# Value rows of a product-key expert layer: scaled and added by VectorE instead of ScalarE and GpSimd

## The chip, the cores and the metric

The kernel runs on one core of a Trainium2 chip. The metric is the device time of one execution in microseconds; lower is better. A run is given as the median of several executions. The profile is one execution, recorded by the hardware profiler; its times are counted from the first instruction. TensorE is called PE in the views, VectorE DVE, ScalarE ACT, GpSimd POOL, and SyncE, which only issues DMAs here, SP.

## The reference, cut to what matters

The program is two transformer blocks on 512 tokens of 1024 features. The change lies in the last part of the second block, a product-key expert layer with 16384 experts: each token takes 8 heads times 16 experts, each with a row of `peer_u` and a row of `peer_v`.

```python
def peer_ffn(h, peer_w_q, peer_keys_1, peer_keys_2, peer_u, peer_v):
    ...
    experts = (e1 * PEER_N_KEYS + e2).reshape(T, PEER_HEADS * PEER_TOPK)
    gates = jax.nn.softmax(sc.astype(jnp.float32), axis=-1)...
    def chunk_fn(args):
        hc, ec, gc = args
        u = peer_u[ec]
        act = jax.nn.gelu(jnp.einsum('cd,ced->ce', hc, u))
        return jnp.einsum('ce,ced->cd', gc * act, peer_v[ec])
...
h = layer_norm(ALPHA * h + peer_ffn(h, ...), ln2_g, ln2_b)
```

## The kernel before

All of the change is in `peer()` and its inner functions. The first 128 tokens are computed as the reference says, from gathered rows: `gather()` fetches, by indirect DMAs issued by GpSimd (L1940), one row for each of the 128 tokens at a time, first 128 times a row of u, then 128 times a row of v. Three row buffers of 128x1024 rotate; row n + 2 is fetched when row n is about to be used. A row of u is multiplied with the tokens and summed by VectorE in one pass (L1953). A row of v is scaled by ScalarE, in place (L1955), and then added to the sum by GpSimd (L1956).

The other 384 tokens go densely through all experts, 128 experts at a time. `up(j)` is a product of 24 matmuls (eight tiles of features, three float32r products each in `mm3`, L281 to L283) that gives the experts' activations (gelu, L1798). `weigh(j)` multiplies them with the gates: the gates lie in DRAM (`gd`, written by the stage before) and are loaded by `gload(c)` for eight j at once, three tiles `page` of 128x1024 for the three tiles of tokens. The multiplication (L1993) is done on VectorE for one tile of tokens at a time, and `split` then makes the exact pair (hi, lo) by a ScalarE copy (L287) and a VectorE subtraction (L288). The products with v run for c = 0 to 15 and, within c, for d = 0 to 7; each is again 24 matmuls, and its sum is added to the residual by `settle` (L2020) on VectorE. 128 such settles count the stage's progress. From c = 1 on each v product is followed by a u product, until the 97 tiles of u that are left are used up: that is a pair, some 97 times, and then single v products to the end.

The weights of every product come as 128x1024 chunks through `Stream`: SP loads them, ScalarE copies the upper part (L155), and the engine in `ws.rest` subtracts it (L157, the lower part, which the third matmul of a triple needs as its weights). In c = 0 `ws.rest` alternates GpSimd and VectorE; from c = 1 it is VectorE. In each d, after `settle`, `next(gat)` advances the gathered rows: by one in c = 0, three in c = 8, else two.

The program is written in this order, but a scheduler orders the instructions of each engine when the kernel is built, by what it holds to be ready; on the chip each engine then runs its instructions in that fixed order. After the last product the last layer norm of the dense tokens ends the program (L1487 to L1509).

Of the kernel before, what the change touches and what calls it, by code (L numbers as in the profile page):

```python
# [14 lines left out]
S = 512  # L15
# [10 lines left out]
# tiles of experts whose act runs beside the queries, the last best keys, the gates, and after them  # L26
# [24 lines left out]
class Arena:  # L51
    """Columns of tiles, given out and taken back in the order of the program."""
# [16 lines left out]
    def alloc(self, n, top=False):  # L69
        """top: for longer than this part of the program."""  # L70
# [35 lines left out]
class Pair:  # L106
    """A float32 array as the exact sum of two float32r arrays."""
# [9 lines left out]
class Stream:  # L117
    """Weights from DRAM in the order of their use: loaded ahead, split ahead.

    The order is what the program asked for when it was traced before (order None: nothing is ahead)."""  # L120
# [20 lines left out]
    def load(self, i):  # L141
        """Chunk i of the order, if there is room."""
        key, n = self.order[i]
        c = self.chunks[key][n]
        if not self.free:
            return False
        c[1] = self.free.pop(0)
        self.k.nc.sync.dma_start(c[1].ap, c[0])
        return True
# [26 lines left out]
    def get(self, key):  # L176
        """The next chunk of that key: (hi, lo), each [128, 1024], or what was loaded. One chunk is used at a time."""
# [31 lines left out]
def drain(*gens):  # L209
    """Runs generators side by side; each yields the time its step takes on the tensor engine."""  # L210
# [11 lines left out]
class K:  # L222
# [6 lines left out]
    # ---- memory  # L229
# [6 lines left out]
    def phase(self, f=0, r=0, turns=True):  # L236
        """The memory that the next part has beside the two arenas: f and r KB. turns: PSUM's banks are used in turn."""
# [40 lines left out]
    # ---- arithmetic  # L278
# [6 lines left out]
    def split(self, hi, lo, x):  # L285
        """hi + lo = x, exactly."""
# [19 lines left out]
    # ---- the program  # L306
# [123 lines left out]
    # ---- modulation: mod[p, tile, kind] = silu(c) @ ada_w + ada_b  # L430
    def ada_prep(self):
# [8 lines left out]
        # the two kinds' silu(c) in the first of 32 columns  # L440
# [3 lines left out]
        # kinds[p, h, k]: whether row p of four products of 32 rows is of half h and of kind k  # L444
# [6 lines left out]
    def ada(self, l, blocks=range(12)):  # L451
# [28 lines left out]
        for nb in blocks:  # L480
            ps = self.bank()
            for ch in range(4):
                w = self.ws.get(f"ada{l}")
                # four products side by side, each on 32 columns of the array: two tiles of features by two halves
# [12 lines left out]
    # ---- norm over features, replicated on all partitions: 1/sqrt(mean(x^2) + eps)  # L497
    def rstd(self, ps, n, cols, eps):
        """ps: sums; gives [128, cols] of 1/sqrt(sum/n + eps)."""
# [6 lines left out]
    def xs(self, k, seg):  # L506
        """Tile k of the residual, some of the tokens: the latents', or the context's from S on."""
# [3 lines left out]
    def tiles(self, h, W):  # L511
        """Tiles of W columns of the two parts of h."""
        return [(h.hi.ap[:, i : i + W], h.lo.ap[:, i : i + W]) for i in range(0, h.hi.n, W)]

    def norm_mod(self, l, j, seg, h):
        """h (tiles): the modulated norm of x, of some of the tokens."""
# [17 lines left out]
    def square(self, x, n, acc):  # L534
        """acc += x^2; acc None: a new one."""
# [9 lines left out]
    def squares(self, x, nk, acc, room):  # L545
        """acc = the sum of x's squared tiles."""
# [6 lines left out]
    def stat(self, k, seg):  # L553
        """Tile k of x is done: its squares are added for the next norm."""
# [3 lines left out]
    def norm(self, x, nk, n, eps=0, acc=None):  # L558
        """1/sqrt(mean over features of x^2 + eps) on all partitions, and two [128, n] to work in."""
# [12 lines left out]
    # ---- the hyena filter's transform at odd frequencies  # L572
    def hy_filter(self):
# [42 lines left out]
        for kind, ts in (("l", range(0, 4)), ("c", range(4, 6))):  # L616
            # h = hid @ w3, decayed: sums and differences of the two sides
# [25 lines left out]
            # 1/(L |h|) by channel  # L643
# [23 lines left out]
    def dft(self, kind, pa, pb, put):  # L667
        """put(f, cos part of pa, sin part of pb), both in PSUM, for each tile of frequencies."""
# [23 lines left out]
    # ---- keys of two heads: tiles 4 and 5 hold one head's each, with zeros in place of the other's features  # L692
# [9 lines left out]
    # ---- layer 0: hyena and windowed attention  # L702
    def mixer0(self, filt):
# [127 lines left out]
        # the tokens of y whose product is done make room for the next norm  # L831
# [899 lines left out]
    def peer(self):  # L1731
# [195 lines left out]
        for x in [keys, iota, sel] + stages + pair:  # L1927
            x.free()
# [584 lines left out]
```

## Time and profile before

| | |
|---|---|
| median of three runs | 4011.34 us (4011.12 to 4017.75) |
| span of the profiled execution | 3998.4 us |
| mean granted TensorE clock | 0.960 of full speed |
| settles of the expert stage (L2020) | 128, from 2903.6 to 3974.0 us |
| rows of u used (L1953) | 128, the last in the window from 3297.7 us |
| adds of rows of v (L1956) | 128, from 3320.1 to 3899.6 us |

The profile lists the span alone for its execution; the median lies 12.9 us above it, which is taken as the start and end around the first and last instruction. The expert stage is thus the last 1100 us, and within it four stretches can be told apart by the count of settles: c = 0 (8 settles, to 2944.8 us), the pairs beside rows of u (40, to 3297.7), the pairs beside rows of v (56, to 3863.1), and the last 24 settles (to 3974.7). The last layer norm takes the rest, to 3998.4.

### The profile page before, as it was taken

How to read it: one execution, taken by the hardware profiler on the slowest of the kernel's cores; microseconds unless marked ns; L12 is line 12 of the kernel's file. 1: busy time of each engine (PE TensorE's matmuls, PEld its weight loads, DVE VectorE, ACT ScalarE, POOL GpSimd, SP SyncE). 2: the span in 40 equal slices, each digit the busy share in tenths (PEclk: the TensorE clock that was granted, in tenths of full speed). 3: DMA queues.
4: the chain of work that ended last, by engine and by line, in shares of the span. 5: the costliest groups of instructions: out<-in, count | busy, mean ns of one | idle time of the engine just before them, and what ended most of it. 6: DMA issues, size and time to landing. Idle time of an engine off the chain costs nothing. (4 is left out here: it accounts for less than half of the span.)

```text
span 3998.4 us, 51340 instructions
## 1 busy us (share of the span) xinstructions
PE 3658.0 (91%) x20063; PEld 3210.7 (80%) x20063; DVE 2703.9 (68%) x4011; ACT 1597.4 (40%) x2504; POOL 1627.3 (41%) x885
## 2 busy tenths in 40 slices
PE   7999999999999999988999888977789998988988
PEld 4766688888878888877888678876788998988987
DVE  6533774434466365557445667999888889899895
ACT  5333452222253333335223554336433334555552
POOL 2222451000042433323001515667754447888880
PEclk8999999999999999999999988989999999999999
DMA  5355432221231222213233313225678887767763
GB/s 196 131 189 195 142 116 77 63 63 63 68 105 56 82 66 79 72 48 106 95 100 101 105 47 126 84 86 162 212 271 295 314 304 240 254 228 239 235 219 99
DMA packets 199599, 573.39 MB, mean 143 GB/s; under 512 B 17051, under 2 KB 67227, under 8 KB 199356
## 3 DMA queue, kind: packets, MB, share of 16 engines
q1 hardware_dynamic: 100224, 362.33, 27.9%
q0 software_dynamic: 49328, 181.73, 12.9%
q10 hardware_dynamic: 49804, 26.06, 2.3%
q8 instruction: 157, 2.57, 0.3%
q14 instruction: 86, 0.70, 0.1%
HBM read 539.64 MB, written 30.41 MB: 143 GB/s over the span
## 5 line engine op out<-in xcount | busy, mean ns | idle before, releaser
L157 POOL TENSOR_TENSOR ra<-fa,ra 128x1024 fp32r<-128x1024 f32 x234 | 591.3, 2533 | 1616.7 <-ACT ra L155 1502.0
L155 ACT CAST ra<-fa 128x1024 fp32r<-128x1024 f32 x591 | 618.0, 1047 | 1293.8 <-PE P L282 499.2
L157 DVE TENSOR_TENSOR ra<-fa,ra 128x1024 fp32r<-128x1024 f32 x357 | 550.2, 1550 | 280.6 <-ACT ra L155 276.7
L282 PE MATMUL P<-ra 128*128 128x512 f32 (+1 forms) x1952 | 700.4, 360 | 10.2 <-DVE ra L288 10.1
L281 PE MATMUL P<-ra 128*128 128x512 f32 (+1 forms) x1824 | 658.0, 367 | 24.9 <-ACT ra L287 14.5
L283 PE MATMUL P<-ra 128*128 128x512 f32 (+1 forms) x1872 | 675.4, 363 | 3.6 <-POOL ra L157 3.6
L283 PE MATMUL bank<-ra 128*128 128x384 f32 (+2 forms) x1648 | 580.6, 353 | 106.1 <-DVE ra L157 81.0
L281 PE MATMUL bank<-ra 128*128 128x384 f32 (+2 forms) x1648 | 578.9, 352 | 10.9 <-DVE fa L1415 4.1
L282 PE MATMUL bank<-ra 128*128 128x384 f32 (+2 forms) x1648 | 572.8, 348 | 2.7 <-DVE ra L288 2.7
L281 PE MATMUL P<-mR,ra 128*128 128x512 f32 (+1 forms) x1344 | 462.9, 348 | 17.9 <-ACT mR L287 8.5
L283 PE MATMUL P<-mR,ra 128*128 128x512 f32 (+1 forms) x1344 | 460.8, 345 | 0.8 <-POOL ra L157 0.7
L282 PEld LDWEIGHTS P<-ra 128*128 128x128 f32 x1952 | 378.6, 194 | 65.7 <-DVE ra L288 12.8
L283 PEld LDWEIGHTS bank<-ra 128*128 128x128 f32 x1648 | 328.5, 199 | 125.4 <-DVE ra L157 94.4
L282 PE MATMUL P<-mR,ra 128*128 128x512 f32 (+1 forms) x1216 | 424.7, 350 | 1.7 <-DVE mR L288 1.7
L281 PEld LDWEIGHTS P<-ra 128*128 128x128 f32 x1824 | 350.5, 194 | 85.2 <-ACT ra L287 16.1
L283 PEld LDWEIGHTS P<-ra 128*128 128x128 f32 x1872 | 360.1, 193 | 58.6 <-POOL ra L157 4.5
L281 PEld LDWEIGHTS bank<-ra 128*128 128x128 f32 x1648 | 328.6, 200 | 16.9 <-ACT ra L155 5.0
L1956 POOL TENSOR_TENSOR fa<-fa 128x1024 f32<-128x1024 f32 x128 | 324.2, 2533 | 25.9 <-ACT fa L1955 23.1
L282 PEld LDWEIGHTS bank<-ra 128*128 128x128 f32 x1648 | 328.2, 199 | 7.0 <-DVE ra L288 3.4
L876 DVE SCALAR_TENSOR_TENSOR fa<-P,fa 128x512 f32<-128x512 f32 (+1 forms) x256 | 163.1, 640 | 224.4 <-PE P L283 223.9
L281 PEld LDWEIGHTS P<-mR,ra 128*128 128x128 f32 x1344 | 258.8, 194 | 54.3 <-ACT mR L287 9.6
L283 PEld LDWEIGHTS P<-mR,ra 128*128 128x128 f32 x1344 | 257.8, 193 | 33.8 <-POOL ra L157 2.7
(421 smaller groups left out, 6315.1 us busy)
## 6 DMA issues: line engine op xcount, KB each, us to landing
fa<-in_w SPq DMA_DIRECT2D x144, 512.0 KB
fa<-in_ud SPq DMA_DIRECT2D x128, 512.0 KB
fa<-in_vd SPq DMA_DIRECT2D x128, 512.0 KB
fa<-in_ada SPq DMA_DIRECT2D x96, 512.0 KB
fa<-in_od_in SPq DMA_DIRECT2D x66, 512.0 KB
gd<-fa ACTq DMA_DIRECT2D x24, 1024.0 KB
page<-gd POOLq DMA_DIRECT2D x48, 512.0 KB
fa<-in_w_q SPq DMA_DIRECT2D x22, 512.0 KB
```

What stands on the lines that cost most here:

```text
L155: self.k.nc.scalar.copy(hi.ap, c[1].ap)
L157: eng.tensor_tensor(lo.ap, c[1].ap, hi.ap.bitcast(F32), op=OP.subtract)
L281: mm(ps, wh, xh, start=start, stop=False)
L282: mm(ps, wh, xl, start=False, stop=False)
L283: mm(ps, wl, xh, start=False, stop=stop)
L876: self.nc.vector.scalar_tensor_tensor(x, ps, g[:, n, kind : kind + 1], x, op0=OP.mult, op1=OP.add)
L1956: nc.gpsimd.tensor_tensor(acc0.ap, acc0.ap, r, op=OP.add)
```

## The change

A row of v is scaled and added by one VectorE instruction. The three gate tiles become one tile `trio` of 128x3072, loaded by one DMA, and the gates are multiplied for all three tiles of tokens by one instruction. `ws.rest` is VectorE from the start of the stage. The rows are advanced in proportion to the products done, 256 rows over 217 products, in place of a fixed number for each d. The pool of `page` tiles is released before the stage, and the `trio` tiles take its place. (Comments were taken out of the file as well; this is left out here.)

```diff
         def page():
-            return pool.tile([128, 1024], F32, name="page", bufs=6)
+            return pages.tile([128, 1024], F32, name="page", bufs=6)
...
+        pages.release()
         for x in [keys, iota, sel] + stages + pair:
             x.free()
...
                 else:
-                    nc.scalar.activation(r, r, AF.Copy, scale=act0.ap[:, n - 128 : n - 127])
-                    nc.gpsimd.tensor_tensor(acc0.ap, acc0.ap, r, op=OP.add)
+                    nc.vector.scalar_tensor_tensor(acc0.ap, r, act0.ap[:, n - 128 : n - 127], acc0.ap, op0=OP.mult, op1=OP.add)
...
+        trios = self.tc.alloc_tile_pool(name="trios", bufs=1, reuse_waits="tile")
+
         def gload(c):
             if c < 16:
-                gbuf[c] = [page() for _ in range(3)]
-                for t in range(3):
-                    nc.gpsimd.dma_start(gbuf[c][t].rearrange("p (b f) -> p b f", f=128), gd[c, :, t * 8 : t * 8 + 8])
+                gbuf[c] = trios.tile([128, 3072], F32, name="trio", bufs=2)
+                nc.gpsimd.dma_start(gbuf[c].rearrange("p (b f) -> p b f", f=128), gd[c])
...
             a = acts.pop(j)
-            for t in range(3):
-                at = a[:, t * 128 : (t + 1) * 128]
-                g = gbuf[j // 8][t].rearrange("p (n e) -> p n e", e=8)[:, :, j % 8]
-                nc.vector.tensor_tensor(at, at, g, op=OP.mult)
+            g = gbuf[j // 8].rearrange("p (n e) -> p n e", e=8)[:, :, j % 8]
+            nc.vector.tensor_tensor(a, a, g, op=OP.mult)
...
-        self.ws.rest = [nc.gpsimd, nc.vector]
+        self.ws.rest = nc.vector
         ws = {}
+        work = 128 + 128 - ahead - 8
+        paced = [0, 0]
+
+        def rows(products):
+
+            paced[0] += products
+            while paced[1] < 256 * paced[0] // work:
+                next(gat, None)
+                paced[1] += 1
...
+                    n = 1
                     if c and ahead < 128:
+                        n = 2
                         up(ahead)
...
-                    for _ in range({0: 1, 8: 3}.get(c, 2)):
-                        next(gat, None)
+                    rows(n)
...
             gload(c + 2)
-            if c == 0:
-                self.ws.rest = nc.vector
```

How the scheduler places the rows is seen in the built programs. On VectorE, where the rows of u end and the rows of v begin, the program before has this (L157 the lower parts of the weights, L1993 the gates, L288 the lower part of the weighed activations, L1953 the rows of u, L1959 the product of the first tile's activations with its gates, L2020 the settles):

```order
L157 TENSOR_TENSOR ra<-fa,ra 128x1024
L1953 SCALAR_TENSOR_TENSOR fa<-fa 128x1024 x2
L157 TENSOR_TENSOR ra<-fa,ra 128x1024
L1993 TENSOR_TENSOR cols<-cols,page 128x128 x3
L288 TENSOR_TENSOR cols<-cols 128x384
L1959 TENSOR_TENSOR fa<-fa 128x128
L2020 SCALAR_TENSOR_TENSOR fa<-fa,bank 128x384
L157 TENSOR_TENSOR ra<-fa,ra 128x1024 x2
L1993 TENSOR_TENSOR cols<-cols,page 128x128 x3
```

The changed program has there (L1956 the rows of u, L1958 the rows of v, L1994 the gates, L1961 the first tile's product, L2021 the settles):

```order
L157 TENSOR_TENSOR ra<-fa,ra 128x1024
L1956 SCALAR_TENSOR_TENSOR fa<-fa 128x1024 x2
L157 TENSOR_TENSOR ra<-fa,ra 128x1024
L1994 TENSOR_TENSOR cols<-cols,trio 128x384
L288 TENSOR_TENSOR cols<-cols 128x384
L1961 TENSOR_TENSOR fa<-fa 128x128
L2021 SCALAR_TENSOR_TENSOR fa<-fa,bank 128x384
L1958 SCALAR_TENSOR_TENSOR fa<-fa 128x1024
L157 TENSOR_TENSOR ra<-fa,ra 128x1024
L1958 SCALAR_TENSOR_TENSOR fa<-fa 128x1024 x2
L157 TENSOR_TENSOR ra<-fa,ra 128x1024
L1994 TENSOR_TENSOR cols<-cols,trio 128x384
```

So rows of v now stand between the lower parts, two or three to a pair, just as the rows of u do, and one gate product stands where three stood. Counted over the whole order, the last row of u comes after 48 settles, the first row of v after 49 and the last after 93; up to there 8 settles have 22 to 24 rows beside them in either kind. In c = 0 13 rows and 7 lower parts stand ahead of the eighth settle, where before 10 and 4 stood.

On GpSimd, the start of the stage reads before (L1901 the last gates, L2012 the residual, L1984 the gate loads, L1940 the row fetches, L157 the lower parts that GpSimd takes):

```order
L1984 DMA page<-gd 128x1024 x2
L1901 TENSOR_TENSOR fa<-fa 128x1024
L2012 TENSOR_TENSOR fa<-ra 128x384 x5
L1940 DMA fa<-in_u,fa 128x1024 x2
L2012 TENSOR_TENSOR fa<-ra 128x384 x3
L1984 DMA page<-gd 128x1024 x4
L1940 DMA fa<-in_u,fa 128x1024
L1984 DMA page<-gd 128x1024 x4
L1940 DMA fa<-in_u,fa 128x1024 x3
L1984 DMA page<-gd 128x1024 x2
L157 TENSOR_TENSOR ra<-fa,ra 128x1024
L1940 DMA fa<-in_u,fa 128x1024 x3
```

and in the changed program (L1903 the last gates, L2013 the residual, L1987 the gate loads, L1943 the row fetches):

```order
L1903 TENSOR_TENSOR fa<-fa 128x1024
L2013 TENSOR_TENSOR fa<-ra 128x384 x5
L1943 DMA fa<-in_u,fa 128x1024 x2
L2013 TENSOR_TENSOR fa<-ra 128x384 x3
L1987 DMA trio<-gd 128x3072 x2
L1943 DMA fa<-in_u,fa 128x1024
L1987 DMA trio<-gd 128x3072
L1943 DMA fa<-in_u,fa 128x1024 x3
```

The first two gate loads moved from ahead of the residual to behind it, and now come with the third tile as one load; the four lower parts of c = 0 are gone from GpSimd.

## Rows read from the trace of the kernel before

**Rows 1.** The page's part 1: busy time, share of the span, instructions

```profile
PE 3658.0 (91%) x20063; PEld 3210.7 (80%) x20063; DVE 2703.9 (68%) x4011; ACT 1597.4 (40%) x2504; POOL 1627.3 (41%) x885
```

**Rows 2.** Windows: PE, PEld, DVE, ACT, POOL busy us (instructions); clock, DMA share, GB/s

```profile
2890.00:2944.80 54.80, 43.25 (x229) 41.65 (x228) 54.28 (x109) 15.89 (x25) 39.04 (x19) 0.90 0.66 238
2944.80:3297.70 352.90, 335.61 (x1868) 330.25 (x1867) 295.05 (x497) 110.52 (x151) 158.13 (x127) 0.98 0.87 303
3297.70:3863.10 565.40, 500.18 (x2685) 490.27 (x2684) 517.01 (x408) 290.82 (x352) 480.10 (x263) 0.94 0.71 239
3863.10:3974.70 111.60, 108.73 (x610) 107.80 (x608) 76.13 (x80) 40.02 (x47) 34.12 (x17) 0.97 0.43 137
```

**Rows 3.** The same windows, of line L2020 (settles) alone

```profile
2944.80:3297.70 352.90, 21.98 (x40) 0.98 0.87 303
3297.70:3863.10 565.40, 30.65 (x56) 0.94 0.71 239
3863.10:3974.70 111.60, 13.27 (x24) 0.97 0.43 137
```

**Rows 4.** Timeline of VectorE near the end (start us, us)

```profile
3910.19 1.29 DVE L1971 SCALAR_TENSOR_TENSOR fa<-fa 128x1024 f32<-128x1024 f32 x1 [0.80 <-DMA fa<-in_ln]
...
3919.94 0.56 DVE L2020 SCALAR_TENSOR_TENSOR fa<-fa,bank 128x384 f32<-128x384 f32 x1 [2.02 <-PE bank L283]
...
3924.10 0.55 DVE L2020 SCALAR_TENSOR_TENSOR fa<-fa,bank 128x384 f32<-128x384 f32 x1 [2.02 <-PE bank L283]
```

**Rows 5.** VectorE's groups, 2944.8 to 3297.7: busy us, mean ns, idle before

```profile
L1953 DVE SCALAR_TENSOR_TENSOR fa<-fa 128x1024 f32<-128x1024 f32 x113 | 137.9, 1223 | 56.0 <-DMA fa<-in_u,fa 55.3
L157 DVE TENSOR_TENSOR ra<-fa,ra 128x1024 fp32r<-128x1024 f32 x78 | 94.9, 1220 | 1.8 <-issue 0.9 <-ACT ra L155 0.9
L1993 DVE TENSOR_TENSOR cols<-cols,page 128x128 f32<-128x128 f32 x120 | 42.0, 404 | 0.0
L2020 DVE SCALAR_TENSOR_TENSOR fa<-fa,bank 128x384 f32<-128x384 f32 x40 | 22.0, 550 | 0.0
```

**Rows 6.** VectorE's groups, 3297.7 to 3863.1

```profile
L157 DVE TENSOR_TENSOR ra<-fa,ra 128x1024 fp32r<-128x1024 f32 x112 | 241.8, 2184 | 41.0 <-ACT ra L155 41.0
L1993 DVE TENSOR_TENSOR cols<-cols,page 128x128 f32<-128x128 f32 x168 | 162.7, 1023 | 1.3 <-ACT cols L1798 1.3
L288 DVE TENSOR_TENSOR cols<-cols 128x384 fp32r<-128x384 f32 x35 | 65.0, 1856 | 0.0
L2020 DVE SCALAR_TENSOR_TENSOR fa<-fa,bank 128x384 f32<-128x384 f32 x56 | 30.6, 547 | 2.1 <-PE bank L283 2.1
```

**Rows 7.** GpSimd's groups, 3297.7 to 3863.1

```profile
L1956 POOL TENSOR_TENSOR fa<-fa 128x1024 f32<-128x1024 f32 x119 | 298.9, 2511 | 21.6 <-ACT fa L1955 19.0
L1940 POOL DMA_INDIRECT fa<-in_vv,fa x122 | 164.1, 1345 | 36.6 <-POOL fa L1956 30.4 <-issue 3.9 <-DVE fa L1953 2.4
```

**Rows 8.** GpSimd's groups, 2944.8 to 3297.7

```profile
L1940 POOL DMA_INDIRECT fa<-in_u,fa x112 | 150.4, 1343 | 196.7 <-DVE fa L1953 189.7 <-issue 3.7 <-DVE cols L1993 2.5
```

**Rows 9.** Waits, 3297.7 to 3863.1: who waited for whom, us, times, longest

```profile
ACT fa L1955 <- DMA fa<-in_vv,fa: 144.6, 70, 4.8
...
PE bank L283 <- DVE ra L157: 60.9, 25, 5.3
DVE ra L157 <- ACT ra L155: 41.0, 20, 5.5
```

**Rows 10.** Waits, 2944.8 to 3297.7

```profile
DVE fa L1953 <- DMA fa<-in_u,fa: 55.3, 43, 5.5
...
PE bank L283 <- DVE ra L157: 16.3, 13, 2.8
```

**Rows 11.** VectorE's groups, 2880 to 2944.8

```profile
L1993 DVE TENSOR_TENSOR cols<-cols,page 128x128 f32<-128x128 f32 x74 | 31.7, 502 | 3.1 <-DMA page<-gd 3.1
```

**Rows 12.** GpSimd's groups, 2880 to 2944.8

```profile
L157 POOL TENSOR_TENSOR ra<-fa,ra 128x1024 fp32r<-128x1024 f32 x4 | 12.8, 3198 | 5.0 <-ACT ra L155 5.0
```

**Rows 13.** Waits, 2880 to 2944.8

```profile
PE bank L283 <- POOL ra L157: 7.6, 1, 7.6
```

More of the change, by code (lines that the diff above doesn't have):

```diff
@@ L1735, in peer @@
         pool = self.mid[0]
+        pages = self.tc.alloc_tile_pool(name="pages", bufs=1, reuse_waits="tile")
         def page():
-            return pool.tile([128, 1024], F32, name="page", bufs=6)
+            return pages.tile([128, 1024], F32, name="page", bufs=6)
         def cols(dt=F32):
@@ L2082, in peer @@
             pass
+        trios.release()
         for x in (acc, ht):
```

## The prediction

> **What bounds the kernel now.** The page's first part [rows 1] has TensorE busy for 91% of the span and VectorE for 68%. That mean hides the stage of the change, so I cut the last 1100 us into stretches by the count of settles and read the windows [rows 2, 3]. Two settles come from a pair (one v product, one settle, and one u product beside it); near the end a settle is one product.
>
> What a product costs when nothing holds it is seen near the end: settles start at 3919.94 and 3924.10, each after VectorE has waited for the matmuls [rows 4]. So 4.16 us is the pace of TensorE, 8.32 a pair. Against that:
> - beside rows of u, 40 settles take 352.9 us: 8.82 a pair, 0.50 over the pace;
> - beside rows of v, 56 settles take 565.4 us: 10.10 a pair, 1.78 over it, or 99 us in all;
> - the last 24 take 111.6 us, 11.8 over the pace, mostly right at their start, where the last rows of v lie.
>
> In the rows-of-v stretch the wait that ends last is TensorE's for the lower part of the weights, L157 [rows 9]: 60.9 us, and the granted clock is 0.94 there against 0.98 before it [rows 2]. Why L157 is late is seen by comparing VectorE's groups of the two stretches [rows 5, 6]. The same instruction takes 1.220 us beside rows of u and 2.184 beside rows of v; the gate product goes from 0.404 to 1.023; the subtraction L288 takes 1.856 where the settle, as wide as it, takes 0.547. The settle itself does not change (0.550 and 0.547). The settle reads one operand from PSUM; the slowed ones read both from SBUF. What is new in that stretch is GpSimd's add, 119 times 2.511 us, 298.9 us of busy time [rows 7]; the row fetches are there in both stretches and as long (1.343 and 1.345) [rows 7, 8]. So VectorE is busy 517 of 565 us [rows 2] largely because it shares something with those adds, and not because it has that much to do. A second wait adds to it: ScalarE waits 144.6 us for rows of v, and the copies that VectorE then needs stand behind (41.0 us) [rows 9].
>
> **The change part by part.**
>
> *Rows of v on VectorE.* Removed: 128 scalings on ScalarE and 128 adds on GpSimd. Added: 128 VectorE instructions of 128x1024 with a scalar. The nearest rows are the same operation without a sum, 1.29 us once [rows 4], and the u rows, 1.223 [rows 5]; I take 1.22. The order has 22 to 24 rows beside 8 settles, 2.9 a pair, as beside rows of u, and the same splits. So the changed stretch is what the stretch beside rows of u already is: two lower parts, 2.9 row instructions, three fetches from DRAM of the same size, one settle, one gate product, no GpSimd arithmetic. I price it by that stretch. VectorE's waits for rows (55.3 us there [rows 10]) come with it, and so does TensorE's 16.3 us wait for L157. Pairs beside rows of v end with settle 93 now.
>
> Here a rule speaks against the change. The Trainium skill, Perfetto Trace Analysis, Optimizing Scalar/DVE Operations, says that work may be offloaded to Scalar or even GPSIMD when DVE is saturated (and adds that DVE and GPSIMD share a read port, so that moving between those two might not help); here work goes to a DVE busy 91% of the stretch. Taken by busy times as they stand, the sum would be 517 plus 119 rows at 1.22 (145) less the saved gate products (163 minus 56 at 0.6, so 129), 533 us, a gain of 32 where the stretch beside rows of u gives 81. I go by the latter, since half of the 517 is slowing [rows 5, 6]: 112 times 0.96 for L157, 163 less 168 times 0.35 for the gates, 35 times 1.3 for L288, together 258.
>
> *One gate product for three.* 120 products take 42.0 us beside rows of u [rows 5], 0.35 each or 1.05 a tile. One of 384 columns costs between 0.55 (a settle, as wide [rows 5]) and 1.05 (nothing gained, if the strided gates set the pace). I take 0.6: 0.45 us less VectorE a pair, 18 us over 40 pairs. VectorE is no bound there (295 of 353 us busy), so only the part that makes L157 earlier counts: between 0 and the 16.3 us that TensorE waits; I take 5, so 8.70 a pair.
>
> *Lower parts of c = 0 by VectorE.* GpSimd's four take 3.198 us each [rows 12], and TensorE waits 7.6 us for one of them [rows 13]. VectorE is busy 54.28 of 54.8 us there [rows 2], so it sets the time: 74 gate products of 31.7 us [rows 11] become 25 at 0.6 (15.0), minus 16.7; 4 more lower parts cost 4.9; 3 more rows ahead of settle 8 cost 3.7. Net minus 8. Against it: the gates of c = 0 now come as one load, issued behind the residual on GpSimd, where two thirds were issued ahead of it; if it lands late, all eight first gate products wait. Bounds: minus 17 (no added work felt) to plus 6 (the load sets the start).
>
> *Paced rows.* The rows end with settle 93, so 12 pairs stand free at about 8.4 us, and the last 24 products at the pace. This costs nothing of its own; DMA traffic stays at some 303 GB/s for longer.
>
> *The sum*, against the span of 3998.4:
> - c = 0: minus 8;
> - 40 pairs beside rows of u: 348 for 352.9, minus 5;
> - 56 pairs: 44 at 8.70 (383) and 12 at 8.4 (101), 484 for 565.4, minus 81;
> - the last 24: 100 for 111.6, minus 11.5.
>
> That is minus 105.5: a span of 3892.9, and with the 12.9 us by which the median lies above the profiled span, **3906 us**. All before the stage stays: the orders of the engines are the same up to it.
>
> **The rivals.**
>
> *A. The gathers become VectorE's wait (3942).* ScalarE's wait of 144.6 us for 120 rows of v is 1.2 us a row; VectorE's for 113 rows of u is 0.5 [rows 9, 10]. If rows of v come later in their own right, VectorE stalls in order with L157 behind it. Its work a pair is 295/40 less 0.45, 6.9 us; with 0.85 us a row (half way) a pair takes 9.4, which gives back 31 us, and 5 more beside rows of u if the load of 1.5 MB in one piece holds up fetches. Against it: beside rows of v each fetch waits for the add of the row before it [rows 7], which explains late rows without a slower DRAM.
>
> *B. TensorE's pace nearly reached (3879).* If the shorter gate product frees VectorE at the right places, 11 us more go beside rows of u and 44 times 0.38 beside rows of v.
>
> *C. VectorE stays slow, and has the rows as well (4120).* If what slows VectorE is the descriptor issue of the fetches and not the adds, L157 stays at 2.18 and the rows, with both large operands in SBUF, take the same: 517/56 (9.2) plus 2.9 rows at 2.18 (6.3) less gate products (1.9) is 13.6 us a pair. Then 44 of them are 598, plus 101, 134 us over now; less the other 24.5 the kernel is slower by 109. It decides above 11.1 us a pair. Against it: as many fetches run beside rows of u, where L157 takes 1.220 [rows 5, 8]. The Trainium skill, SBUF — State Buffer, Who interferes with whom, says the same: a DVE instruction with two SBUF inputs contends with a GpSimd instruction that reads SBUF, not with one that only writes it.
>
> *D. Nothing moves (4011).* It would need TensorE to be held in the rows-of-v stretch by something else of the same size, such as the weights' loads; DMA is busy 0.71 there and 0.87 in the faster stretch [rows 2], so I see none.
>
> **How the numbers follow.** The forecast has 0.63, A 0.20, B 0.12, C 0.03, D 0.02. Less than 0.2% (8 us) can hardly be told from no change in a measurement of this kernel; the forecast, A and B are far beyond it: faster 0.95, same 0.02, slower 0.03. The range: from 3872 (pace reached in all of it and 6 us more at the start, 34 below the forecast) to 3955 (A with 13 us more at the start, where the gate load is late), leaving out C, D and the ends of A and B.
>
> **What would show it.** Right: L157 near 1.22 us throughout the stage; rows of v near 1.22; TensorE's wait for L157 under 25 us between settles 48 and 93; pairs of 8.5 to 8.9 us; the last row some 200 us ahead of the last product; the granted clock near 0.98. Wrong: VectorE's wait for in_vv above 1 us a row (A); L157 or the rows near 2 us without a GpSimd add beside them (C); a first settle later than 2904 (the gate load). The prediction falls if pairs beside rows of v stay above 9.5 us.

## The result, and the profile after

The changed kernel takes **3937.57 us** (median of four runs, 3935.89 to 3942.07), against 4011.23 of the kernel before: a ratio of 0.9819, 95% interval 0.9805 to 0.9833. It is faster, by 74 us, where the prediction had 105. The profiled execution has a span of 3934.4 us.

The page's part 1 of the kernel after (as [rows 1]):

```profile
PE 3624.5 (92%) x20063; PEld 3181.3 (81%) x20063; DVE 2552.2 (65%) x3887; ACT 1467.2 (37%) x2378; POOL 1275.6 (32%) x721
```

VectorE has 128 row instructions of 1024 columns more, and is busy 152 us less. That is the first sign that much of its work before was waiting inside instructions.

The windows of the kernel after, cut at settles 8, 48, 93, 104 and 128 (columns as in [rows 2]). Rows of v now end with settle 93, so there are two stretches where [rows 2] has one:

```profile
2949.00:3304.40 355.40, 339.55 (x1907) 333.71 (x1907) 292.04 (x421) 113.33 (x154) 151.69 (x118) 0.99 0.87 305
3304.40:3714.60 410.20, 385.94 (x2152) 377.04 (x2150) 343.32 (x360) 129.90 (x181) 185.52 (x135) 0.98 0.87 304
3714.60:3803.10 88.50, 88.50 (x512) 88.50 (x512) 53.81 (x66) 37.03 (x54) 0.55 (x1) 1.00 0.45 149
3803.10:3909.70 106.60, 106.60 (x616) 106.52 (x615) 52.12 (x68) 28.80 (x34) 0.00 (x0) 1.00 0.29 94
```

40 settles beside rows of u take 355.3 us (352.9 before, [rows 3]), 45 beside rows of v 410.2 (9.12 a pair, 10.10 before), 11 free pairs 88.5, and the last 24 settles 106.6. The 56 pairs together are 498.7 us where they were 565.4. From before to after, the span changes by +4.8 us up to settle 8, +2.4 beside rows of u, -66.7 in the 56 pairs, -5.0 in the last 24 and +0.4 behind them: -64.

VectorE's groups of the kernel after, 3304.4 to 3714.6 (columns as in [rows 5]; answers [rows 6]):

```profile
L1958 DVE SCALAR_TENSOR_TENSOR fa<-fa 128x1024 f32<-128x1024 f32 x127 | 163.0, 1284 | 66.0 <-DMA fa<-in_vv,fa 64.4
L157 DVE TENSOR_TENSOR ra<-fa,ra 128x1024 fp32r<-128x1024 f32 x90 | 109.6, 1220 | 0.0
L1994 DVE TENSOR_TENSOR cols<-cols,trio 128x384 f32<-128x384 f32 x45 | 40.9, 910 | 0.0
L2021 DVE SCALAR_TENSOR_TENSOR fa<-fa,bank 128x384 f32<-128x384 f32 x46 | 25.3, 550 | 0.0
L288 DVE TENSOR_TENSOR cols<-cols 128x384 fp32r<-128x384 f32 x26 | 14.5, 557 | 0.0
```

The lower part L157 takes 1.220 us where it took 2.184, the subtraction L288 0.557 where it took 1.856. The settle, which was not slowed, stays at 0.550. But the gate product L1994 takes 0.910, and VectorE stands 64.4 us before its rows of v, 0.5 us a row.

The waits of the kernel after, 3304.4 to 3714.6 (answers [rows 9]):

```profile
POOL fa L1943 <- DVE fa L1958: 193.2, 106, 6.8
DVE fa L1958 <- DMA fa<-in_vv,fa: 64.4, 52, 3.6
...
PE bank L283 <- DVE ra L157: 20.9, 18, 2.9
```

And beside rows of u, 2949 to 3304.4 (answers [rows 10]):

```profile
POOL fa L1943 <- DVE fa L1956: 197.2, 103, 6.8
DVE fa L1956 <- DMA fa<-in_u,fa: 63.1, 52, 2.9
...
PE bank L283 <- DVE ra L157: 12.1, 11, 2.8
```

The stretch beside rows of v has become much like the one beside rows of u, as the prediction said: nearly the same clock (0.98 and 0.99), DMA share (0.87 in both) and wait (64.4 and 63.1 us). In both the order of events is now: GpSimd waits for VectorE to be done with a row buffer, fetches into it, VectorE waits for the landing, and the next L157 stands in order behind that row.

How many rows these three buffers give can be worked out. In this stretch a fetch lands 7.05 us after it is issued in the mean (median 6.6, from 4.5 to 11.9); the 1.42 us that it takes on GpSimd are part of that. The row instruction takes 1.28, and the next fetch into the buffer starts 0.36 us behind it. That makes 8.7 us a round, so by this estimate three buffers give a row each 2.9 us at best, and the 2.9 rows of a pair ask for 8.4 us: TensorE's own pace of 8.3, with nothing to spare for landings that vary so much. VectorE used 129 rows in 410.2 us, one each 3.2; the 0.86 us that a round takes longer are rows that have landed and stand until VectorE comes to them. (The expectations of 4, 6 and 11 below have 3.05 to 3.1 us a row; 11 tells how: the fetch's own time was added to a landing that already holds it.)

### The profile page after: what moved, and what is told of

It is laid out like the page before. It is cut to its first block, busy times and chain, and to the rows that moved or that the text cites. A ratio compares the mean times of both kernels' runs of the same rounds, so it can differ in the third digit from the quotient of the medians.

```text
span 3934.4 us, 51004 instructions
## 1 busy us (share of the span) xinstructions
PE 3624.5 (92%) x20063; PEld 3181.3 (81%) x20063; DVE 2552.2 (65%) x3887; ACT 1467.2 (37%) x2378; POOL 1275.6 (32%) x721
## 5 line engine op out<-in xcount | busy, mean ns | idle before, releaser
L155 ACT CAST ra<-fa 128x1024 fp32r<-128x1024 f32 x591 | 619.4, 1050 | 1487.4 <-PE bank L282 644.4
L157 POOL TENSOR_TENSOR ra<-fa,ra 128x1024 fp32r<-128x1024 f32 x230 | 578.8, 2522 | 1605.3 <-ACT ra L155 1478.0
L157 DVE TENSOR_TENSOR ra<-fa,ra 128x1024 fp32r<-128x1024 f32 x361 | 443.4, 1229 | 282.0 <-ACT ra L155 279.6
L283 PE MATMUL bank<-ra 128*128 128x384 f32 (+2 forms) x1648 | 569.4, 346 | 60.5 <-DVE ra L157 43.1
L281 PE MATMUL bank<-ra 128*128 128x384 f32 (+2 forms) x1648 | 568.8, 346 | 12.0 <-ACT ra L287 5.5
L282 PE MATMUL bank<-ra 128*128 128x384 f32 (+2 forms) x1648 | 562.7, 342 | 8.3 <-DVE ra L288 8.3
L283 PEld LDWEIGHTS bank<-ra 128*128 128x128 f32 x1648 | 320.1, 194 | 78.6 <-DVE ra L157 55.7
L281 PEld LDWEIGHTS bank<-ra 128*128 128x128 f32 x1648 | 320.5, 195 | 17.3 <-ACT ra L287 6.1
L282 PEld LDWEIGHTS bank<-ra 128*128 128x128 f32 x1648 | 320.2, 194 | 12.7 <-DVE ra L288 9.2
L281 PEld LDWEIGHTS P<-mR,ra 128*128 128x128 f32 x1344 | 258.4, 193 | 54.8 <-ACT mR L287 10.4
L283 PEld LDWEIGHTS P<-mR,ra 128*128 128x128 f32 x1344 | 257.8, 193 | 33.9 <-issue 2.4
L282 PEld LDWEIGHTS P<-mR,ra 128*128 128x128 f32 x1216 | 232.9, 192 | 32.1 <-DVE mR L288 2.4
```

What stands on the lines that cost most here:

```text
L155: self.k.nc.scalar.copy(hi.ap, c[1].ap)
L157: eng.tensor_tensor(lo.ap, c[1].ap, hi.ap.bitcast(F32), op=OP.subtract)
L281: mm(ps, wh, xh, start=start, stop=False)
L282: mm(ps, wh, xl, start=False, stop=False)
L283: mm(ps, wl, xh, start=False, stop=stop)
```

## The experiments

All times of settles are starts of L2020 or what stands for it, in the profiled execution; "a pair" is the mean over settles 8 to 104, 96 pairs in every kernel (a pair gives one settle). One execution alone can be some us off: the 40 pairs beside rows of u took 348.7 us in 1 and 349.3 in 8, whose edits don't touch them, where before has 352.9 and after 355.3.

| kernel | median us | ratio (95%) | settle 8 | a pair | settle 128 |
|---|---|---|---|---|---|
| before | 4011.2 | 1 | 2944.2 | 9.57 | 3974.0 |
| after | 3937.6 | 0.9819 (0.9805 to 0.9833) | 2949.0 | 8.90 | 3909.6 |
| 1 rows only | 3931.1 | 0.9805 (0.9778 to 0.9833) | 2946.1 | 8.88 | 3905.5 |
| 2 add only | 3972.2 | 0.9904 (0.9878 to 0.9931) | 2954.1 | 9.28 | 3951.9 |
| 3 rest only | 4002.9 | 0.9997 (0.9985 to 1.0008) | 2951.3 | 9.52 | 3976.0 |
| 4 held | 4235.3 | 1.0557 (1.0524 to 1.0589) | 2952.5 | 11.81 | 4214.3 |
| 5 idle adds | 4056.0 | 1.0133 (1.0115 to 1.0151) | 2952.0 | 10.06 | 4024.7 |
| 6 ordered | 3873.2 | 0.9672 (0.9656 to 0.9688) | 2945.3 | 8.31 | 3849.3 |
| 7 ordered, 4 buffers | 3867.3 | 0.9659 (0.9641 to 0.9676) | 2941.6 | 8.28 | 3843.1 |
| 8 early gates | 3934.0 | 0.9823 (0.9807 to 0.9840) | 2947.5 | 8.88 | 3907.0 |
| 9 gates in runs | 3919.9 | 0.9793 (0.9777 to 0.9810) | 2929.0 | 8.84 | 3885.0 |
| 10 all that helped | 3857.6 | 0.9640 (0.9622 to 0.9659) | 2929.5 | 8.28 | 3831.1 |
| 11 four buffers | 3885.9 | 0.9695 (0.9672 to 0.9719) | 2942.7 | 8.41 | 3856.7 |

The first three take the change apart. **1** is the kernel before with the row edit alone:

```diff
-                    nc.scalar.activation(r, r, AF.Copy, scale=act0.ap[:, n - 128 : n - 127])
-                    nc.gpsimd.tensor_tensor(acc0.ap, acc0.ap, r, op=OP.add)
+                    nc.vector.scalar_tensor_tensor(acc0.ap, r, act0.ap[:, n - 128 : n - 127], acc0.ap, op0=OP.mult, op1=OP.add)
```

> The kernel before with one edit alone: rows of v scaled and added by VectorE in one instruction. Theory (GpSimd's adds slow VectorE's instructions with both operands in SBUF, and that made the rows-of-v stretch slow): the lower parts L157 take 1.22 us in all of the stage, the pairs beside rows of v fall from 10.1 to about 9.0 us, and the edit gives nearly all of the gain: 3940 us, ratio 0.980 to 0.986. Rival (the three gate products and the split lower parts of the start carry a good part of it): ratio 0.988 or more, with pairs above 9.4 us.

It gives all of the gain: 0.9805 (0.9778 to 0.9833), beside 0.9819 of the whole change. A pair beside rows of v (settles 49 to 94) takes 9.16 us, about as in after. L157 in it, 3300 to 3700:

```profile
L157 DVE TENSOR_TENSOR ra<-fa,ra 128x1024 fp32r<-128x1024 f32 x87 | 105.9, 1221 | 2.4 <-ACT ra L155 2.4
```

**2** is the kernel before with the add alone moved; the scaling stays on ScalarE:

```diff
-                    nc.gpsimd.tensor_tensor(acc0.ap, acc0.ap, r, op=OP.add)
+                    nc.vector.tensor_tensor(acc0.ap, acc0.ap, r, op=OP.add)
```

> The kernel before with the scaling of the rows of v left on ScalarE, and only the add moved from GpSimd to VectorE. Theory (GpSimd's add is the cause): L157 back to 1.22 us, pairs beside rows of v at 9.0 to 9.4 us, ratio below 0.988. Rival (ScalarE's wait for the gathered rows, 144.6 us in the kernel before, with the copies of the weights queued behind it, is the cause): ScalarE still waits for the rows, the copies come late, and the ratio stays above 0.993 whatever L157 takes.

VectorE's groups and the waits of this kernel, 3350 to 3750:

```profile
L1956 DVE TENSOR_TENSOR fa<-fa 128x1024 f32<-128x1024 f32 x113 | 138.2, 1223 | 81.2 <-ACT fa L1955 80.7
L157 DVE TENSOR_TENSOR ra<-fa,ra 128x1024 fp32r<-128x1024 f32 x81 | 98.8, 1220 | 17.2 <-ACT ra L155 17.2
```

```profile
ACT fa L1955 <- DMA fa<-in_vv,fa: 166.4, 69, 7.6
DVE fa L1956 <- ACT fa L1955: 80.7, 49, 5.6
```

Without GpSimd's adds L157 is at 1.220 though ScalarE still scales the rows, so the slowing is gone in full. Yet only half the gain is there (0.96% of 1.95%), and a pair beside rows of v (settles 49 to 95) takes 9.86 us, more than the theory's 9.0 to 9.4. The ratio of 0.9904 lies between theory and rival. What is lost is lost by the scaling on ScalarE: it waits for a landing before each one, 166.4 us in 400, with the upper parts (L155) behind it in order, and VectorE waits for it in turn. But this wait is not the one of the kernel before. The 80.7 us that VectorE stands before the scaled rows are new, since GpSimd took that wait before, and VectorE's wait for the upper parts fell to 17.2 us in 400 (41.0 in 565 before, [rows 9]). How the gain splits between GpSimd's adds and ScalarE's queue as they stood before is not shown.

**3** is the changed kernel with ScalarE's scaling and GpSimd's adds put back (the diff of 1, reversed):

> The changed kernel with the rows of v given back to ScalarE and GpSimd, so the gates in one tile, the lower parts of the start on VectorE and the pacing alone. Theory: these move little; the start costs 5 us, one gate product of 0.9 us saves little beside rows of u; beside GpSimd's adds one product in place of three waits for them less often, some 10 us; ratio 0.995 to 1.001. Rival (they are half of the gain): ratio 0.992 or less.

0.9997 (0.9985 to 1.0008): the one gate product, the lower parts of c = 0 and the paced rows give nothing together while GpSimd has the adds.

**4** tried to take away the early fetches: in the changed kernel GpSimd copies a settled column into the row buffer before each fetch, so that a row can't be fetched long before its place.

```diff
                 if n < 256:
+                    if mark:
+                        nc.gpsimd.tensor_copy(rows[n % 3].ap[:, 0:1], mark[0])
...
             ps.free()
+            mark[:] = [av[:, d, c0 : c0 + 1]]
```

> The changed kernel with each fetch of a row held until the settle before it in the program is done, by a GpSimd copy of one settled column into the row buffer, so that rows do run at 256 over 217 products (2.3 to 2.4 a pair in the built order, and not 2.9). Theory (the pairs stand at 8.9 to 9.1 us because VectorE waits in order for rows that come one in 3.05 us, the pace of three buffers, and the lower parts stand behind it): the pairs fall to 8.4 to 8.6 us, the rows end near settle 120, 3900 to 3915 us, ratio 0.972 to 0.977. Rival (VectorE's load or TensorE's own pace with its clock sets the pairs): pairs stay at 8.8 or more, and the stage is as long or longer, 3935 us or more.

1.0557: the edit missed its aim. The fetch now starts late, but the row instruction follows soon behind it in VectorE's order, so each landing is waited for; the waits, 3400 to 3700:

```profile
POOL fa L1944 <- DVE fa L2024: 123.0, 23, 10.7
DVE fa L1960 <- DMA fa<-in_vv,fa: 68.9, 14, 6.8
...
DVE fa L1958 <- DMA fa<-in_u,fa: 61.8, 12, 7.5
PE bank L283 <- DVE ra L157: 56.7, 22, 5.2
```

5 us for each wait, where after has 1.2. It shows what a late fetch costs, and nothing on what the fetches cost where they stand.

**5** gives the changed kernel GpSimd adds that feed nothing (the output doesn't depend on them), one behind each fetch of v, to see what adds alone do to VectorE:

```diff
-                    nc.gpsimd.indirect_dma_start(out=rows[n % 3].ap, out_offset=None, in_=self.a["u" if n < 128 else "vv"],
+                    got = nc.gpsimd.indirect_dma_start(out=rows[n % 3].ap, out_offset=None, in_=self.a["u" if n < 128 else "vv"],
...
+                    if n >= 128:
+                        with self.tc.issue_after(got.ins):
+                            nc.gpsimd.tensor_tensor(junk, ht.ap, ht.ap, op=OP.add)
```

> The changed kernel, which keeps its rows on VectorE, with one more GpSimd add of 128x1024 behind each fetch of a row of v; what it adds up is used by nothing. Theory (GpSimd's adds hold what VectorE's instructions with two operands in SBUF need): L157 goes back above 1.8 us beside rows of v, the VectorE rows too, pairs of 10 us or more, 3990 us or more (ratio to the kernel before 0.995 or more), since VectorE now has the rows as well. Rival (the adds themselves were harmless and ScalarE's queue made the stretch slow): L157 stays at 1.22 us and the ratio at 0.982.

VectorE's groups, 3350 to 3750, and GpSimd's:

```profile
L1962 DVE SCALAR_TENSOR_TENSOR fa<-fa 128x1024 f32<-128x1024 f32 x98 | 188.5, 1924 | 4.4 <-DMA fa<-in_vv,fa 3.9
L157 DVE TENSOR_TENSOR ra<-fa,ra 128x1024 fp32r<-128x1024 f32 x74 | 128.4, 1737 | 0.0
L1998 DVE TENSOR_TENSOR cols<-cols,trio 128x384 f32<-128x384 f32 x37 | 47.0, 1270 | 0.0
L288 DVE TENSOR_TENSOR cols<-cols 128x384 fp32r<-128x384 f32 x22 | 22.8, 1038 | 0.0
L2025 DVE SCALAR_TENSOR_TENSOR fa<-fa,bank 128x384 f32<-128x384 f32 x36 | 19.6, 544 | 0.0
```

```profile
L1948 POOL TENSOR_TENSOR junk<-fa 128x1024 f32<-128x1024 f32 x80 | 171.1, 2138 | 1.9
```

80 adds on other buffers, which VectorE never waits for, bring the slowing back: L157 from 1.220 to 1.737, the rows from 1.284 to 1.924, the gates from 0.910 to 1.270; the settle, with one operand in PSUM, stays at 0.544. That is a little under the 1.8 us expected for L157, and under the 2.184 of before, where the adds fill 53% of the stretch and not 43%. VectorE is busy 395.6 of the 400 us, has almost no wait for rows left (3.9 us) and is the bound; a pair beside rows of v (settles 48 to 95) takes 10.97 us. (To make room this kernel has one tile fewer in the `cols` pool; so have 7, 10 and 11, which are among the four shortest.)

**6** aims at the wait that is left. The scheduler puts a row into VectorE's order as soon as it holds it ready, 22 to 24 beside 8 settles. Here each row may stand only behind the settle that precedes it in the program:

```diff
-            nc.vector.scalar_tensor_tensor(x, x, ALPHA if c == 0 else 1.0, ps.ap[:, : c1 - c0], op0=OP.mult, op1=OP.add)
+            mark[:] = [nc.vector.scalar_tensor_tensor(x, x, ALPHA if c == 0 else 1.0, ps.ap[:, : c1 - c0], op0=OP.mult, op1=OP.add).ins]
...
-                next(gat, None)
+                if mark:
+                    with self.tc.issue_after(mark[0]):
+                        next(gat, None)
+                else:
+                    next(gat, None)
```

> The changed kernel with each row's VectorE instruction queued behind the settle that stands before it in the program, by an order edge without a wait, so that 19 rows instead of 22 to 24 stand beside 8 settles, and the fetches as free as before. Theory (the rows come one in 3.05 us from three buffers, 2.9 a pair ask for 8.9 us; 2.36 a pair ask for 7.2): VectorE's wait for rows falls below 0.2 us a row, pairs to 8.4 to 8.6 us, the last row near settle 120, 3900 to 3915 us, ratio 0.973 to 0.977. Rival (VectorE's load or TensorE's clock sets the pairs, whatever the rows do): pairs stay above 8.75 and the time within 10 us of 3937.

0.9672, 64 us less than the changed kernel and 27 less than the theory's own range: pairs come at 8.31 us, below its 8.4, and settle 8 comes 3.7 us earlier, with 9 rows ahead of it and not 13. Now 19 rows stand beside 8 settles, 2.4 a pair, the last behind settle 119. The window and the waits of this kernel, 3300 to 3700:

```profile
3300.00:3700.00 400.00, 399.03 (x2303) 398.71 (x2302) 335.23 (x374) 138.83 (x193) 185.75 (x119) 1.00 0.85 296
```

```profile
DVE fa L1958 <- DMA fa<-in_vv,fa: 26.1, 22, 3.9
DVE fa L2022 <- PE bank L283: 19.3, 26, 1.2
```

TensorE is busy 399 of 400 us, at a granted clock of 1.00, and VectorE now waits for TensorE. Its wait for rows of v is 26.1 us, 0.3 a row, and not below 0.2, but it no longer holds TensorE. 115 rows in 400 us are one each 3.5 us, slower than the 2.9 that three buffers can give.

**7** adds a fourth row buffer to 6 (one tile in `trios`, one fewer in `cols`; the fetch goes three rows ahead in place of two):

> As the run with rows queued behind settles, with a fourth row buffer (and one column tile less to make room). Theory (a row's path of fetch issue, some 7 us to landing, and use is what three buffers can't hide): a fourth buffer takes the rest of VectorE's waits for rows, 5 to 15 us less than with three. Rival (DRAM traffic at 87% is the limit): the waits do not change, and neither does the time.

0.9659 (0.9641 to 0.9676), an interval that overlaps that of 6. VectorE's waits for rows fall to 4.1 us in 3300 to 3700, but TensorE was at its pace already, so the pairs gain 0.03 us; 3.7 of the 6 us lie ahead of settle 8. The window, 3300 to 3700:

```profile
3300.00:3700.00 400.00, 400.00 (x2310) 400.00 (x2309) 336.39 (x371) 139.18 (x193) 181.89 (x119) 1.00 0.85 296
```

**11** has the fourth buffer without the order; in short (the buffers are taken in turns of four, and `cols` has one tile fewer):

```diff
-            rows = [self.F(D) for _ in range(3)]
+            rows = [self.F(D) for _ in range(3)] + [trios.tile([128, D], F32, name="row", bufs=1)]
...
-                fetch(n + 2)
+                fetch(n + 3)
```

> The changed kernel with four row buffers instead of three and nothing else: its rows still stand as early in VectorE's order as they do in the changed kernel. Theory (three buffers set the rows' rate: a landing of 6.7 us and a row instruction of 1.28 us after it, and the fetch itself, divided by three buffers is 3.1 us a row, and 2.9 rows a pair at that rate are 9.0 us): with four the rows could come each 2.4 us, so VectorE's wait for in_vv falls under 20 us, pairs beside rows fall to 8.4 us, and the whole gains 40 to 65 us over the changed kernel, a ratio of 0.965 to 0.972. Rival (the places of the rows in the order set it: whatever can land early is placed early, VectorE stalls just the same): waits for rows of 50 us or more remain, pairs stay above 8.9, a ratio of 0.979 to 0.983.

0.9695 (0.9672 to 0.9719): the gain over the changed kernel is 52 us, in the theory's range. The waits, 3300 to 3700:

```profile
DVE fa L1962 <- DMA fa<-in_vv,fa: 26.3, 20, 3.7
DVE ra L157 <- ACT ra L155: 24.4, 16, 2.9
...
DVE fa L1962 <- DMA row<-in_vv,fa: 10.4, 8, 3.7
PE bank L283 <- DVE ra L157: 8.8, 9, 2.4
```

Three things were off. The wait for rows is 36.7 us (0.33 a row, 0.5 in after), not under 20. A pair beside rows of v is 8.77 us (settles 46 to 88), not 8.4. And the places did not stay: the scheduler now puts 23 to 25 rows beside 8 settles throughout, so that the last stands behind settle 88 and not 93. So a fourth buffer gives 52 us although the rows stand even earlier, and fewer rows a pair (6) give 64 with three buffers. Either takes most of the loss away; a share for each can't be told.

**8** writes `gload(0)` ahead of the residual, since GpSimd's adds of the residual stand before it in its queue:

```diff
+        gload(0)
         ht = self.F(D, top=True)
...
-        gload(0)
         gload(1)
```

> The changed kernel with the first gate load written ahead of the residual, so that GpSimd issues it some 3 us earlier. Theory (the first eight products wait for the one load of three tiles): settle 8 comes 3 to 4 us earlier than in the changed kernel (2949.0 us), and the total by as much. Rival (VectorE's work in c = 0 sets it): settle 8 within 1 us.

0.9823, no gain; settle 8 is 1.5 us earlier, between theory and rival and within what one execution is off. The load moves from 2874.69 to 2871.82 only. It stands behind the last write of gates to DRAM, which ScalarE issues at 2865.24 in after and which takes 5.0 us to land. Nor did it land earlier: VectorE's first gate product, which waits for it, starts at 2883.70 here and at 2883.75 in after. Why is open.

**9** lays the gates out so that a product reads 16 tokens side by side, where it reads one in eight:

```diff
-            nc.scalar.copy(stage.v(16, 16, 8).rearrange("p c t j -> p t c j")[:, half * 4 : half * 4 + 4],
+            nc.scalar.copy(stage.v(16, 8, 16).rearrange("p c j t -> p t c j")[:, half * 4 : half * 4 + 4],
...
-            g = gbuf[j // 8].rearrange("p (n e) -> p n e", e=8)[:, :, j % 8]
-            nc.vector.tensor_tensor(a, a, g, op=OP.mult)
+            g = gbuf[j // 8].rearrange("p (b e n) -> p b e n", e=8, n=16)[:, :, j % 8]
+            a3 = a.rearrange("p (b n) -> p b n", n=16)
+            nc.vector.tensor_tensor(a3, a3, g, op=OP.mult)
```

> The changed kernel with the gates laid out in DRAM so that the product reads them in runs of 16 columns instead of one column in eight. Theory (the step of 32 bytes makes the gate product take 0.91 us where 384 columns side by side take 0.55): the product falls to 0.55 to 0.65 us, settle 8 comes 5 to 10 us earlier because VectorE sets the pace of c = 0, and the time falls by about as much; beside the rows little changes, since there the rows' arrival sets the pairs. Rival (the product's 0.91 us is not the step): the product stays at 0.9 us and the time within 3 us of 3937.

VectorE's groups of this kernel, 3300 to 3700:

```profile
L1958 DVE SCALAR_TENSOR_TENSOR fa<-fa 128x1024 f32<-128x1024 f32 x125 | 160.4, 1283 | 78.9 <-DMA fa<-in_vv,fa 78.2
...
L1995 DVE TENSOR_TENSOR cols<-cols,trio 128x384 f32<-128x384 f32 x44 | 24.3, 553 | 0.0
```

The product takes 0.553 us where it took 0.910. Beside rows the time saved turns into a longer wait for rows (78.2 us where after has 62.2 in the same window), and a pair beside rows of v stays at 9.08 (9.12 in after): VectorE's work is no bound there. It pays in c = 0, where VectorE has little slack (busy 61.35 of the 65.25 us from the first gate product to settle 8 in after): the 30 gate products up to settle 8 take 14.7 us instead of 24.8. Settle 8 is 20 us earlier, but 7.6 of that are there before the gates: the first copy of the gate stage (L1879) starts at 2677.2 in this profile and at 2684.8 in that of after. The copy itself, which now writes apart, goes from 0.585 to 1.06 us, hidden in ScalarE's waits for TensorE. The intervals of 9 and after just overlap, and with the 7.6 us in it the gain of 9 is not certain.

**10** is 7 with 8 and 9, to see whether the parts add up:

> Rows queued behind settles, four row buffers, the first gate load early, gates in runs of 16: the edits that gave something, together. Theory: beside the rows TensorE is at its pace already, so the rest comes from c = 0 alone, 5 to 12 us less than the run with four buffers (3867 us): 3855 to 3862. Rival (c = 0 waits for the gate load and the first rows, not for VectorE): 3865 us or more.

3857.6 us, 0.9640 (0.9622 to 0.9659), the shortest of all and in the theory's range. The window of it, 3300 to 3700:

```profile
3300.00:3700.00 400.00, 400.00 (x2309) 400.00 (x2309) 319.75 (x369) 139.29 (x193) 169.04 (x118) 1.00 0.85 296
```

TensorE has no gap left beside the rows; settle 8 comes at 2929.5, 12 us ahead of 7 (whose gate stage started 2.9 us later). The interval touches that of 7.

## Why the prediction was right, and what was mis-sized

The direction, the cause and the range (3872 to 3955) came true. The forecast of 3906 itself was 31.6 us short, and rival A's 3942 lies nearer to the 3937.6 measured. Of the signs named ahead, L157 (1.220), TensorE's wait for it (20.9 us), the place of the last row and the clock (0.98) came; the pairs of 8.5 to 8.9 us did not (9.12), and the sign of a late gate load did (first settle at 2913.5). Where the prediction says that two settles come from a pair, one does, and its sums go by one.

**What bounds the kernel.** Right: VectorE was slow, not overloaded, and what slowed it was the GpSimd adds (L157 at 2.184 with them, 1.220 without in 1, 2 and after, 1.737 with idle ones in 5). The Trainium skill, SBUF — State Buffer, Who interferes with whom, says that a VectorE instruction with two SBUF inputs contends with a GpSimd instruction that reads SBUF. By that rule L157, L288, the gates and the rows must slow and the settle must not; the traces of before and of 5 agree, with 0.547 and 0.544 us for the settle. The prediction called ScalarE's wait for the rows an addition. 2, which keeps the scaling there, has only half the gain, so the scaling had to go as well; whether that wait weighed as much before is not shown. The sum doesn't hang on it, since the edit removes both and the price was the stretch beside rows of u, which has neither.

**The offload rule** of the Trainium skill (Perfetto Trace Analysis, Optimizing Scalar/DVE Operations) points the other way from this change, and the sum by busy times gave a gain of 32 us. Measured: 74 us for the whole, and the row edit alone does no worse (0.9805). Going by the stretch beside rows of u was right: work moved onto the engine that was busy 91% left it less busy (343.3 of 410.2 us, 84%).

**The 56 pairs** (484 forecast, 498.7 measured, 14.7 over). 45 beside rows took 9.12 each, not 8.70. Three sizes failed here. The gate product was priced at 0.6 us, "between 0.55 and 1.05"; it is 0.910, near the upper bound, so that one for three saves 0.14 us of VectorE's time and not 0.45 (three took 1.05 [rows 5]). The row was priced at 1.22 and takes 1.284, the 1.29 of the other row that the prediction named. And neither mattered as the prediction thought: 9 gives the 0.55, and a pair beside rows of v stays at 9.08. What holds a pair is rival A's mechanism, the gathers, in a milder form (0.5 us a row and not 0.85), and at work beside rows of u as well, where the prediction read the 55.3 us wait as a cost that comes along and not as the bound. A hint was in the trace before, which has no landing times of these fetches: 113 rows in 352.9 us [rows 5] are one each 3.1 us, with VectorE waiting for them. 6 and 7 remove that and reach 8.3 to 8.4 a pair, 11 most of it. So rival B's 8.3 a pair was within reach, but by way of the buffers and the rows' places, not by the gate product. The 11 free pairs took 8.04 each (8.4 forecast), 4 us on the good side. TensorE was no faster there: 512 matmuls in 88.5 us are 4.15 a product, the pace of [rows 4], and part of the pairs' products fell behind settle 104.

**40 pairs beside rows of u** (348 forecast, 355.3 measured). The 5 us were to come from the shorter gate product. VectorE waited 63.1 us for rows there (55.3 before), so time saved on it had nowhere to show. No gain is seen; with 348.7 us in 1 and 349.3 in 8 for the same pairs, 5 us can't be told from scatter here.

**c = 0** (minus 8 forecast, plus 4.8 measured). The upper bound's cause, the gate load, was the right one: the first settle comes at 2913.5, later than the 2904 that the prediction named, at 2915.7 in 3, which has the one load too, and at 2905.0 in 1, which has three. Of the 4.8 us at settle 8 some may be scatter (1, whose c = 0 is that of before, has 1.9). VectorE's timeline shows how, first of before and then of after:

```profile
2862.78 9.33 DVE L1993 TENSOR_TENSOR cols<-cols,page 128x128 f32<-128x128 f32 x16 [4.06 <-DMA page<-gd]
```

```profile
2869.72 1.23 DVE L157 TENSOR_TENSOR ra<-fa,ra 128x1024 fp32r<-128x1024 f32 x1 [10.51 <-ACT ra L155]
...
2883.75 6.20 DVE L1994 TENSOR_TENSOR cols<-cols,trio 128x384 f32<-128x384 f32 x8 [4.49 <-DMA trio<-gd]
```

Before, the gates of two thirds of the tokens were loaded while the last third was still being written, and 16 of their products (9.3 us) ran in a gap of VectorE. The one load for all is issued behind the last write, so that work moved from the gap into the stretch where VectorE sets the time. The prediction counted the products after 2880 alone, 74, and so saved 16.7 us where 31.7 became 24.8. TensorE stands too: from 2884 to 2896 it is busy 3.96 of 12 us at a mean granted clock of 0.53, in before 11.13 at 0.72. 8 shows that an earlier place of the load in the program doesn't help.

**The last 24** (100 forecast, 106.6 measured, TensorE busy throughout). The count was wrong here: between settles 104 and 128 TensorE runs 616 matmuls, 25.7 products at 4.15 us, and not 24. One of them belongs to the 97th pair, which the prediction's 96 pairs leave out, and part of another to the 96th. [Rows 2] had 610 in that stretch, 25.4 products, which at the pace are 106 of its 111.6 us; so the last rows of v, to which the prediction laid most of the 11.8 us over the pace, cost about half of them. The gain of 5 us is real: 1 has 106.5 us too, and 3, with GpSimd's adds, 110.4.

**Paced rows, and the 12.9 us.** The pacing changes little in the order: in 1, which has the old fixed numbers, 10, 30, 54, 76, 100 and 122 rows stand before settles 8, 16, 24, 32, 40 and 48, and in after 13, 33, 57, 79, 103 and 126. So 20 to 24 stand beside 8 settles either way, because the scheduler takes a row when it holds it ready. The span was forecast 41.5 us too short. The 12.9 us for start and end were 9.7 too many (3.2 after), because the profiled execution of before was shorter than its median: in the profiled execution after, the time lies 1.7 us above the span, and later runs of before lie between 3997 and 4014. By luck these 9.7 us hide part of the 41.5.

**Rivals C and D** fell: L157 at 1.220 with as many fetches, and DMA busy 0.87 in the faster stretch.

Open: why a fourth buffer still leaves 36.7 us of waits in 11; a run with five buffers wasn't tried. Why the gate stage starts up to 16.1 us apart in kernels whose edits lie behind its start (2677.2 in 9 to 2693.3 in 4) isn't known either; it limits what 9 and 10 can say of single terms.

## What to carry to other kernels

An engine that is busy 91% may be slow instead of full: compare the mean time of the same instruction with and without its neighbour's work before moving work off it, and look for an instruction with another kind of operand that did not slow. When a wait for a rotating buffer remains, divide landing plus use by the buffers (the issue is in the landing already) and hold it against the uses per step of the engine that should be the bound, with room for landings that vary; a fourth buffer or fewer uses per step was worth 52 to 64 us here, a shorter gate product 18 at most. Before joining several loads into one, see which of them started before the last of their data was written.

## What the runs showed of the hardware

- One VectorE product of 384 columns whose second operand takes one float in eight took 0.910 us, and 0.553 with 16 floats side by side; three of 128 columns with one in eight took 0.404 each, and 1.05 of busy time together.
- ScalarE's copy of 512 columns from PSUM took 0.585 us, and 1.06 when what it wrote lay apart for the layout of 9.
- GpSimd's indirect fetches of 128 rows of 4 KB land 6.6 (rows of v) to 7.0 us (rows of u) after issue (medians in after; 4.4 to 15.1 in all), and with three buffers one came each 3.1 to 3.2 us.
- Beside GpSimd adds of 128x1024 that fill 43% of a stretch (5), VectorE's instructions with both operands in SBUF took 1.4 to 1.9 times as long (L157 1.737 for 1.220, L288 1.038 for 0.557), and the settle with one operand in PSUM 0.544 us as without them.
